# A hybrid decoder block on one core: first partial w2 sums stored from ScalarE's queue, rope tables one stretch later and wholly on VectorE, latent weights split earlier

## The chip, the cores and the metric

The kernel runs on one core of a Trainium2 chip. TensorE (PE) multiplies, VectorE (DVE) and ScalarE (ACT) prepare its operands and read its sums, GpSimd (POOL) and SyncE (SP) mostly issue transfers. The metric is the device time of one execution in microseconds; the reported time is the median of several executions.

## The reference, cut to what matters

One layer: a gated FFN, a mixer (latent attention beside a short convolution), and a second gated FFN, each behind an RMS norm modulated by an adaLN vector and each added to the residual. x is 512 x 1024 in f32; the FFN's inner width is 2816 (22 tiles of 128).

```python
h = modulate(x, norm_w[l, 0], mod[:, 0, 0], mod[:, 0, 1])
x = x + 0.5 * mod[:, 0, 2][:, None, :] * swiglu(h, ffn_w13[l, 0], ffn_w2[l, 0])
h = modulate(x, norm_w[l, 1], mod[:, 1, 0], mod[:, 1, 1])
y = hybrid_mixer(h, cos, sin, w_in[l], ...)        # starts with h @ w_in; its first columns are the latents
x = x + mod[:, 1, 2][:, None, :] * y
...
cos, sin = rope_tables(positions)                  # used in the mixer alone
```

## The kernel before, in words

All products run in f32 precision as three matmuls of split operands: `split_to` makes a rounded high part on ACT (L112) and the rest on DVE (L113). Every weight that PE multiplies by has first been loaded by SP into a raw tile and then split by these two lines.

An FFN (`ffn`) is a list of jobs that `run` goes through: while the body of job i issues PE's work, the splits of job i+1 (`prep`) are woven in at its yields, and the loads of job i+2 (`load`) are issued at its start. The first three of the 22 inner tiles are done ahead of the list; a `pair_job` does one of the others from the two w13 tiles with seven products; it needs sums of weight parts, and it gets two of these by accumulating loads on POOL's queue (L537, L538) on top of parts that SP loaded (L536). A `down_job` multiplies by w2. The inner tiles come in three phases; in the first FFN they are 0 to 5, 6 to 13 and 14 to 21, and after each phase comes a w2 stretch of eight output tiles. The first stretch stores its partial sums to a scratch array `yd` (L676 copy on ACT, L680 store), the second adds to them by an accumulating store (L678), the last fetches them back and puts the sum into the residual (`Residual.put`, L368). In the last stretch of the first FFN the output tiles 4 to 7 are done for the first half of the rows and then for the second half, with their split weights kept, so that the norm of the next part (`Norm.add`, `rstd`, `spread`, `chunk`) can start on the first half while PE is at the second.

Beside this run the adaLN products on DVE (L199), whose weights come in 1 MB blocks (L227). `rope_tables` (L740 to L779) is called in the first w2 stretch after tile 0: a scaling of one column, 20 small DVE instructions, two sines on ACT, and eight multiplications on POOL (L777). The weights of the mixer's first product (the latents, `w_c`) are loaded and split after the whole FFN in the program text (L809 to L815). Then the mixer starts with `latent_products(0)` (L840) and the norm's second half.

SBUF is cut into 17 blocks of 8 KB per partition (tag `block`), five slots of 2 KB (`slot`), ten tiles of 4 KB (`wide`) and others. Tiles of one tag take turns: a load waits until the one that it replaces was last read. A `block` holds, among others, a weight load of a job, 1 MB of adaLN weights, two activations, a split latent weight, and `rope_tmp`. The order of each engine's instructions is set ahead of time by the framework's planner, from the program's order, the data that they need and the tiles that are free; on the chip every engine then goes through its list in that order.

Of the kernel before, what the change touches and what calls it, by code (L numbers as in the profile page):

```python
# [9 lines left out]
F32R = mybir.dt.float32r  # L10
# [3 lines left out]
ALU = mybir.AluOpType  # L14
# [44 lines left out]
def tile_hybrid_block(ctx, tc, xT, pack0, pack1, pos, ada01, ada, w13f0, w13f1, w13a, w13b, w2, w_c, w_cg, w_uq, w_ukv,  # L59
# [17 lines left out]
    def block(name, dt=F32):  # L77
        return act.tile([P, 4 * T], dt, tag="block", name=name, bufs=NBLOCK)
# [28 lines left out]
    def cols(pair, c0, n):  # L107
        return tuple(t[:, c0 : c0 + n] for t in pair)
# [6 lines left out]
    def raw_load(src, n, name):  # L115
        raw = wide(f"wr_{name}") if section["kind"] == "ffn" else short("wr", WMAX, f"wr_{name}")
        nc.sync.dma_start(out=raw[:, :n], in_=src)
        return raw
# [367 lines left out]
    def first_raw(i, early):  # L486

        n = FIRST[i] * 2 * P
        per = (4 * T if early else WMAX) // n
        for k in range(KD):  # L490
            if k % per == 0:
                t = block(f"wfr{i}_{k}") if early else wide(f"wfr{i}_{k}")
            raw = t[:, k % per * n : (k % per + 1) * n]
            nc.sync.dma_start(out=raw, in_=(w13f0, w13f1)[i][k])
            yield raw

    def ffn(i, norm, spans, chunk, res, next_norm, pace, raws):
        a_pieces = {}
        ab = []
        yd = dram.tile([KD, P, T], F32, name=f"yd{i}")  # L500
# [118 lines left out]
        def down_job(phase, ms, halves, keep=False):  # L619


            f0, f1 = PHASES[i][phase]
            n = f1 - f0
            final = phase == len(PHASES[i]) - 1
            name = f"d{i}_{phase}_{ms[0]}_{halves[0]}"
            first_half = halves[0] == 0

            def load(w):
                if not first_half:
                    return  # L630
                w["raw"] = block(f"wd{name}")
                for z, m in enumerate(ms):
                    nc.sync.dma_start(out=w["raw"][:, z * WMAX : z * WMAX + n * P], in_=w2[i, m][:, f0 * P : f1 * P])
                if final:
                    for m in ms:
                        res.fetch(m)
                        nc.sync.dma_start(out=res.part[m], in_=yd[m])

            def prep(w):
                if not first_half:  # L640
                    return
                if not final:
                    ada_load(ADA[i][phase])
                elif ms[0] == 0:
                    res.room()
                for z, m in enumerate(ms):
                    raw = w["raw"][:, z * WMAX : z * WMAX + n * P]
                    if keep:
                        b = block(f"{name}_{m}", F32R)
                        kept[m] = b[:, : n * P], b[:, WMAX : WMAX + n * P]  # L650
                        split_to(*kept[m], raw)
                    else:
                        split_wide(w, raw, (m,), f"{name}_{m}", False)
                    yield
                if final:
                    for m in ms:
                        nc.vector.scalar_tensor_tensor(out=res.xin[m], in0=res.part[m], scalar=mod_col(res.v, m),
                                                       in1=res.xin[m], op0=ALU.mult, op1=ALU.add)

            def body(w):  # L660
                for m in ms:
                    ps = mm(f"{name}_{m}")
                    wt = w.get(m) or kept[m]
                    if not first_half and next_norm is not None:
                        for _ in range(next(pace_of)):
                            next(next_norm.steps, None)
                    for k in range(n):
                        for h in halves:
                            c = h * HALF
                            mm3(ps[:, c : c + HALF], cols(wt, k * P, P), cols(a_pieces[f0 + k], c, HALF),  # L670
                                k == 0 and h == halves[0], k == n - 1 and h == halves[-1])
                        if k == n // 2:
                            yield
                    if not final:
                        y = slot(f"y{name}_{m}")
                        nc.scalar.copy(out=y, in_=ps)  # L676
                        if phase:
                            nc.gpsimd.dma_start(out=yd[m], in_=y, accum_op=ALU.add)  # L678
                        else:
                            nc.gpsimd.dma_start(out=yd[m], in_=y)  # L680
                        ada_step(ADA[i][phase] // len(ms))
                        if i == phase == m == 0:
                            rope_tables()
                    else:
                        c, k = halves[0] * HALF, len(halves) * HALF
                        res.put(m, ps[:, c : c + k], c, k)
                        if next_norm is not None:
                            next_norm.add(m, c, k)
                            if m == KD - 1:
                                drain(next_norm.steps)  # L690
                                next_norm.steps = next_norm.prepare(c // P, k // P)
                    yield

            return load, prep, body
# [44 lines left out]

    def rope_tables():  # L740
        nc.vector.tensor_scalar(out=wq96, in0=wq96, scalar1=SCALE, scalar2=None, op0=ALU.mult)
        rope_tmp = block("rope_tmp")

        def rope_tile(i):
            return rope_tmp[:, 64 * i : 64 * i + 64].rearrange("p (b f) -> p b f", f=16)

        posf = rope_tmp[:, 448 : 448 + NB]
        nc.vector.tensor_copy(out=posf, in_=pos_i)
        ang = rope_tile(0)
        for b in range(NB):  # L750
            nc.vector.tensor_scalar(out=ang[:, b, :], in0=invf, scalar1=posf[:, b : b + 1], scalar2=None, op0=ALU.mult)
        TWO_PI = 6.283185307179586
        C1, C2 = 6.28125, 0.0019340515136718750
        C3 = TWO_PI - C1 - C2
        MAGIC = 12582912.0
        trig = {}
        for name, quarter in (("sin", 0.0), ("cos", 0.25)):
            kk = rope_tile(1 + 3 * len(trig))
            nc.vector.tensor_scalar(out=kk, in0=ang, scalar1=1.0 / TWO_PI, scalar2=quarter, op0=ALU.mult, op1=ALU.add)
            nc.vector.tensor_scalar(out=kk, in0=kk, scalar1=MAGIC, scalar2=None, op0=ALU.add)  # L760
            nc.vector.tensor_scalar(out=kk, in0=kk, scalar1=MAGIC, scalar2=None, op0=ALU.subtract)
            r = rope_tile(2 + 3 * len(trig))
            nc.vector.scalar_tensor_tensor(out=r, in0=kk, scalar=-C1, in1=ang, op0=ALU.mult, op1=ALU.add)
            nc.vector.scalar_tensor_tensor(out=r, in0=kk, scalar=-C2, in1=r, op0=ALU.mult, op1=ALU.add)
            nc.vector.scalar_tensor_tensor(out=r, in0=kk, scalar=-C3, in1=r, op0=ALU.mult, op1=ALU.add)
            if quarter:
                nc.vector.tensor_scalar(out=r, in0=r, scalar1=TWO_PI / 4, scalar2=None, op0=ALU.add)
            nc.vector.tensor_scalar(out=r, in0=r, scalar1=3.1415925, scalar2=-3.1415925, op0=ALU.min, op1=ALU.max)
            tb = rope_tile(3 + 3 * len(trig))
            nc.scalar.activation(out=tb, in_=r, func=AF.Sin)  # L770
            trig[name] = tb

        for nm, w in (("q", wqr_sb), ("k", wkr_sb)):
            for fn in ("cos", "sin"):
                tb = const.tile([P, NB, DR], F32, name=f"rt_{nm}{fn}")
                for j in range(2):
                    nc.gpsimd.tensor_tensor(out=tb[:, :, 16 * j : 16 * j + 16], in1=trig[fn], op=ALU.mult,  # L777
                                            in0=w[:, 16 * j : 16 * j + 16].unsqueeze(1).to_broadcast([P, NB, 16]))
                rope_tab[nm, fn] = tb  # L779

# [21 lines left out]
    x2d = dram.tile([KD, P, T], F32, name="x2d")  # L802
    r1 = Residual(1, xT, 2, x1d)
    n1 = Norm(1, r1.tiles)
    ffn(0, n0, ((0, T),), first_chunk, r1, n1, (0, 2, 3, 3), first_raw(0, False))

    wc = []  # L809
    for u in range(4):  # L810
        raw = raw_load(w_c[u], 2 * CPROJ, f"wc{u}")
        hl = block(f"wc{u}", F32R)
        hl = hl[:, : 2 * CPROJ], hl[:, 2 * CPROJ : 4 * CPROJ]
        split_to(*hl, raw[:, : 2 * CPROJ])
        wc += [cols(hl, i * CPROJ, CPROJ) for i in range(2)]  # L815
    enter("mixer")
    kr_raw = act.tile([P, NB, DR], F32, name="kr_raw")
    cst = act.tile([P, NB, 4], F32, name="cst")
# [426 lines left out]
```

## Time and profile before

| | us |
|---|---|
| median of 3 runs | 1089.38 (1087.56 to 1100.96) |
| the profiled execution | 1097.2 |
| its span, first to last instruction | 1095.4 |
| PE busy in it | 1046.0 |
| mean granted clock of PE | 0.991 |

Of the profiled execution 1.8 us lie outside its span. The profiled execution is 7.8 us longer than the median of the runs. The rows below are from that one execution; their times are in microseconds from the span's start. In its order of work the first FFN's first w2 stretch lies at about 99 to 132 us, its second at 220 to 264, its third at 345 to 389, and the mixer starts at 389.5.

### The profile page before, as it was taken

What the parts mean: (1) busy time and instruction counts of PE and PEld (TensorE: products, weight loads), DVE (VectorE), ACT (ScalarE), POOL (GpSimd) and SP (SyncE); (2) the same over time, 40 slices, a digit from 0 to 9 for tenths busy, and PEclk for the clock granted to TensorE, in tenths of its full rate; (3) what the DMA queues carried; (4) which work ended last, traced back from release to release, by engine and by line L of the source; (5) the groups of instructions that cost most, each with busy time, mean ns of one, the idle gap of its engine ahead of it and who ended that gap; (6) DMA issues with size and microseconds to landing.
All of it is one profiled execution on the core that took longest, in us unless ns stands there. A gap on an engine that the chain in (4) does not pass through costs nothing.

```text
span 1095.4 us, 19960 instructions
## 1 busy us (share of the span) xinstructions
PE 1046.0 (95%) x7870; PEld 982.7 (90%) x7870; DVE 782.3 (71%) x1326; ACT 513.9 (47%) x877; POOL 135.7 (12%) x169
## 2 busy tenths in 40 slices
PE   2999989999999989999999989899999999999997
PEld 1999989999999988888887868688999999999997
DVE  6899389855987577767468677648997488834863
ACT  7964345423554154554334433327764255524530
POOL 0001311013100112110000000001101220022001
PEclk9999999999999989999999999899999999999999
DMA  9766987579945423212245486725866894778352
GB/s 367 249 191 197 267 246 206 193 178 272 238 122 205 152 101 97 83 54 68 78 151 187 131 297 235 242 95 155 211 196 223 231 248 128 210 138 216 99 195 85
DMA packets 82254, 198.08 MB, mean 181 GB/s; under 512 B 9584, under 2 KB 12528, under 8 KB 79088
## 3 DMA queue, kind: packets, MB, share of 16 engines
q1 hardware_dynamic: 66256, 164.30, 44.8%
q0 software_dynamic: 15904, 32.51, 15.3%
q8 instruction: 61, 1.00, 0.4%
q14 instruction: 33, 0.27, 0.1%
HBM read 178.95 MB, written 17.83 MB: 180 GB/s over the span
## 4 chain that ended last, share of the span: by engine, by line
PE 76%; DVE 10%; DMA 7%; issue 3%; ACT 1%; SPq 1%; POOL 1%; POOLq 0%; DVEq 0%; ACTq 0%
PE g L134 6%; PE g L135 6%; PE g L136 6%; PE d L135 6%; PE d L136 6%; PE d L134 6%; PE u L134 5%; PE u L135 5%; PE u L136 5%; DMA sa<-in_w13a_dram 2%; DMA wr_ada<-in_ada_dram 2%; DVE ada_acc L199 2%; PE pf L135 1%; PE pf L136 1%; PE pf L134 1%
## 5 line engine op out<-in xcount | busy, mean ns | idle before, releaser
L135 PE MATMUL d<-a,d_h 128*128 128x256 f32 x616 | 171.4, 278 | 1.6 <-DVE a L113 1.6
L136 PE MATMUL d<-a,d_l 128*128 128x256 f32 x616 | 170.9, 278 | 0.0
L134 PE MATMUL d<-a,d_h 128*128 128x256 f32 x616 | 170.9, 278 | 0.0
L134 PE MATMUL u<-T,w_h 128*128 128x256 f32 x456 | 127.8, 280 | 4.0 <-ACT s L567 4.0
L135 PE MATMUL u<-T,w_h 128*128 128x256 f32 x456 | 127.3, 279 | 0.0
L136 PE MATMUL u<-T,w_l 128*128 128x256 f32 x456 | 127.2, 279 | 0.0
L112 ACT CAST w_h<-sa 128x1024 fp32r<-128x1024 f32 x76 | 79.8, 1050 | 81.7 <-issue 48.5
L135 PEld LDWEIGHTS d<-a,d_h 128*128 128x128 f32 x616 | 115.7, 188 | 2.1 <-DVE a L113 2.1
L136 PEld LDWEIGHTS d<-a,d_l 128*128 128x128 f32 x616 | 116.0, 188 | 0.0
L134 PEld LDWEIGHTS d<-a,d_h 128*128 128x128 f32 x616 | 115.9, 188 | 0.0
L113 DVE TENSOR_TENSOR w_l<-sa,w_h 128x1024 fp32r<-128x1024 f32 x76 | 92.5, 1220 | 20.5 <-ACT w_h L112 10.8
L134 PEld LDWEIGHTS u<-T,w_h 128*128 128x128 f32 x456 | 86.2, 189 | 4.9 <-ACT s L567 4.8
L136 PEld LDWEIGHTS u<-T,w_l 128*128 128x128 f32 x456 | 86.7, 190 | 0.0
L135 PEld LDWEIGHTS u<-T,w_h 128*128 128x128 f32 x456 | 86.1, 189 | 0.0
L134 PE MATMUL g<-h,w_h 128*128 128x256 f32 x304 | 84.6, 278 | 0.0
L135 PE MATMUL g<-h,w_h 128*128 128x256 f32 x304 | 84.4, 278 | 0.0
L136 PE MATMUL g<-h,w_l 128*128 128x256 f32 x304 | 84.4, 278 | 0.0
L112 ACT CAST d_h<-wdd 128x1024 fp32r<-128x1024 f32 (+1 forms) x42 | 41.0, 978 | 57.6 <-issue 31.3
L547 DVE TENSOR_TENSOR sb<-sa 128x512 f32<-128x512 f32 x38 | 26.0, 684 | 53.7 <-DMA sa<-in_w13a_dram 32.6
L113 DVE TENSOR_TENSOR d_l<-wdd,d_h 128x1024 fp32r<-128x1024 f32 (+1 forms) x42 | 47.7, 1135 | 16.8 <-ACT d_h L112 11.2
L113 DVE TENSOR_TENSOR w_l<-sb,w_h 128x1024 fp32r<-128x1024 f32 x38 | 46.4, 1220 | 17.5 <-PE g L136 13.5
L136 PEld LDWEIGHTS g<-h,w_l 128*128 128x128 f32 x304 | 57.4, 189 | 0.0
(362 smaller groups left out, 3131.6 us busy)
## 6 DMA issues: line engine op xcount, KB each, us to landing
ada<-in_ada_dram SPq DMA_DIRECT2D x24, 1024.0 KB, 6.7
sa<-in_w13b_dram SPq DMA_DIRECT2D x80, 256.0 KB, 5.0
sa<-in_w13a_dram SPq DMA_DIRECT2D x72, 256.0 KB, 5.3
wdd<-in_w_dram SPq DMA_DIRECT2D x32, 512.0 KB, 4.7
wr_ada<-in_ada_dram SPq DMA_DIRECT2D x24, 512.0 KB, 5.1
sa<-in_w13b_dram POOLq DMA_DIRECT2D x40, 256.0 KB, 6.1
sa<-in_w13a_dram POOLq DMA_DIRECT2D x36, 256.0 KB, 6.3
yd<-yd POOLq DMA_DIRECT2D x32, 256.0 KB, 6.1
```

Of the source, the lines that this page charges most:

```text
L112: nc.scalar.copy(out=hi, in_=src)
L113: nc.vector.tensor_tensor(out=lo, in0=src, in1=hi.bitcast(F32), op=ALU.subtract)
L134: nc.tensor.matmul(ps, a[0], b[0], start=first, stop=False, skip_group_check=parts)
L135: nc.tensor.matmul(ps, a[0], b[1], start=False, stop=False, skip_group_check=parts)
L136: nc.tensor.matmul(ps, a[1], b[0], start=False, stop=last, skip_group_check=parts)
L199: nc.vector.scalar_tensor_tensor(out=acc, in0=src, scalar=c, in1=acc, op0=ALU.mult, op1=ALU.add)
L547: nc.vector.tensor_tensor(out=b[:, 0], in0=a[:, 3], in1=a[:, 1], op=ALU.add)
```

## The change

Three edits, all of them in the first FFN or in `ffn`, which the second FFN uses too.

- The stores of the first w2 stretch (both FFNs, eight each) are issued by ACT instead of POOL.
- `rope_tables` is called one w2 stretch later (the first FFN's second, after tile 0); its scratch is a `slot` instead of a `block`; its eight last multiplications go from POOL to DVE.
- The latent weights' loads and splits become a generator that the FFN steps: after each of the four first-half `put`s of the last stretch one weight tile is split; the four loads come at the first step.

```diff
-    def ffn(i, norm, spans, chunk, res, next_norm, pace, raws):
+    def ffn(i, norm, spans, chunk, res, next_norm, pace, raws, tail=iter(())):
...
                         if phase:
                             nc.gpsimd.dma_start(out=yd[m], in_=y, accum_op=ALU.add)
                         else:
-                            nc.gpsimd.dma_start(out=yd[m], in_=y)
+                            nc.scalar.dma_start(out=yd[m], in_=y)
                         ada_step(ADA[i][phase] // len(ms))
-                        if i == phase == m == 0:
+                        if i == 0 and phase == 1 and m == 0:
                             rope_tables()
                     else:
                         c, k = halves[0] * HALF, len(halves) * HALF
                         res.put(m, ps[:, c : c + k], c, k)
+                        if len(halves) == 1 and first_half:
+                            next(tail, None)
...
-        rope_tmp = block("rope_tmp")
+        rope_tmp = slot("rope_tmp")
...
-                    nc.gpsimd.tensor_tensor(out=tb[:, :, 16 * j : 16 * j + 16], in1=trig[fn], op=ALU.mult,
+                    nc.vector.tensor_tensor(out=tb[:, :, 16 * j : 16 * j + 16], in1=trig[fn], op=ALU.mult,
...
-    ffn(0, n0, ((0, T),), first_chunk, r1, n1, (0, 2, 3, 3), first_raw(0, False))
     wc = []
-    for u in range(4):
-        raw = raw_load(w_c[u], 2 * CPROJ, f"wc{u}")
-        hl = block(f"wc{u}", F32R)
-        hl = hl[:, : 2 * CPROJ], hl[:, 2 * CPROJ : 4 * CPROJ]
-        split_to(*hl, raw[:, : 2 * CPROJ])
-        wc += [cols(hl, i * CPROJ, CPROJ) for i in range(2)]
+    def latent_weights():
+        raws = [raw_load(w_c[u], 2 * CPROJ, f"wc{u}") for u in range(4)]
+        for u, raw in enumerate(raws):
+            hl = block(f"wc{u}", F32R)
+            hl = hl[:, : 2 * CPROJ], hl[:, 2 * CPROJ : 4 * CPROJ]
+            split_to(*hl, raw[:, : 2 * CPROJ])
+            wc.extend(cols(hl, i * CPROJ, CPROJ) for i in range(2))
+            yield
+
+    ffn(0, n0, ((0, T),), first_chunk, r1, n1, (0, 2, 3, 3), first_raw(0, False), latent_weights())
```

## Rows read from the trace of the kernel before

**Rows 1.** The page, part 1: PE's busy time, share of the span, instructions.

```profile
PE 1046.0 (95%) x7870; PEld 982.7 (90%) x7870; DVE 782.3 (71%) x1326; ACT 513.9 (47%) x877; POOL 135.7 (12%) x169
```

**Rows 2.** Windows: stretch, length, busy us by engine, PE's clock, DMA share, GB/s.

```profile
85.00:103.00 18.00, 17.68 (x156) 17.48 (x155) 16.64 (x36) 7.80 (x12) 0.00 (x0) 1.00 0.56 191
122.00:135.00 13.00, 13.00 (x113) 13.00 (x113) 5.04 (x6) 6.27 (x10) 5.04 (x8) 1.00 1.02 288
146.00:149.60 3.60, 0.00 (x0) 0.00 (x0) 2.85 (x6) 0.86 (x2) 0.00 (x0) 1.00 1.02 315
149.60:153.40 3.80, 3.79 (x19) 3.79 (x20) 2.15 (x3) 1.57 (x2) 0.79 (x1) 0.55 1.08 309
...
103.00:135.00 32.00, 32.00 (x275) 32.00 (x274) 15.35 (x29) 11.55 (x19) 14.26 (x22) 1.00 0.90 262
```

**Rows 3.** Chain that ended last, 90 to 160: start, us, what.

```profile
114.28 12.51 DMA sa<-in_w13a_dram
...
148.27 0.35 DVE g L585
...
149.29 0.27 ACT s L567
149.61 0.47 PE u L134
```

**Rows 4.** Timeline of DVE: start, length, instruction, [idle before, what ended it].

```profile
122.49 0.69 DVE L547 TENSOR_TENSOR sb<-sa 128x512 f32<-128x512 f32 x1 [9.18 <-DMA sa<-in_w13a_dram]
...
135.08 0.69 DVE L547 TENSOR_TENSOR sb<-sa 128x512 f32<-128x512 f32 x1 [3.00 <-DMA sa<-in_w13a_dram]
```

**Rows 5.** Timeline of POOL.

```profile
111.11 0.94 POOL L537 DMA_DIRECT2D sa<-in_w13a_dram  x1
```

**Rows 6.** Timeline of SP's queue.

```profile
97.16 0.33 SPq L227 DMA_DIRECT2D ada<-in_ada_dram  x1
103.28 1.75 SPq L536 DMA_DIRECT2D sa<-in_w13a_dram  x4
...
110.59 0.33 SPq L227 DMA_DIRECT2D ada<-in_ada_dram  x1
```

**Rows 7.** Waits of SP's queue: us in total, times, longest.

```profile
SPq L227 <- POOL rt_kcos L777: 3.1, 1, 3.1
```

**Rows 8.** Tile rope_tmp: ns min/median/max, first to last start.

```profile
L763 DVE SCALAR_TENSOR_TENSOR rope_tmp<-rope_tmp x2: 210/210/211, 104.2 to 104.4; 128x64 f32<-128x64 f32 x2
...
L777 POOL TENSOR_TENSOR rt_kcos<-pk,rope_tmp x2: 768/769/770, 109.1 to 109.8; 128x64 f32<-128x64 f32 x2
```

**Rows 9.** Line L536: SP's issues, ns min/median/max.

```profile
L536 SPq DMA_DIRECT2D sa<-in_w13a_dram x72: 327/430/1812, 40.6 to 300.0; - x72
```

**Rows 10.** Windows of the second w2 stretch and of the second FFN's first.

```profile
225.00:240.00 15.00, 15.00 (x130) 15.00 (x129) 3.94 (x5) 3.45 (x5) 4.42 (x5) 1.00 0.92 173
...
845.00:885.00 40.00, 40.00 (x356) 40.00 (x355) 21.37 (x28) 13.23 (x19) 12.71 (x17) 1.00 0.91 261
```

**Rows 11.** Windows at the end of the first FFN and the mixer's start.

```profile
368.00:380.00 12.00, 12.00 (x102) 12.00 (x102) 5.01 (x10) 1.67 (x4) 2.16 (x4) 1.00 0.24 88
...
389.80:392.20 2.40, 0.06 (x1) 0.00 (x0) 2.40 (x6) 2.40 (x5) 0.54 (x1) 0.98 0.00 0
392.20:399.40 7.20, 7.14 (x23) 6.88 (x24) 4.00 (x7) 0.55 (x2) 0.71 (x1) 0.53 0.64 239
```

**Rows 12.** Tile wc: the splits' ns min/median/max, first to last start.

```profile
L112 ACT CAST wc<-wr_wc x4: 870/872/882, 387.2 to 391.0; 128x832 fp32r<-128x832 f32 x4
L113 DVE TENSOR_TENSOR wc<-wr_wc,wc x4: 1011/1015/1015, 391.2 to 395.1; 128x832 fp32r<-128x832 f32 x4
```

**Rows 13.** Timeline of PE at the mixer's start.

```profile
389.51 0.35 PE L134 MATMUL pc<-wc,h 128*128 128x416 f32 x1
392.25 0.71 PE L135 MATMUL pc<-wc,h 128*128 128x416 f32 x1 [2.40 <-DVE wc L113]
...
394.50 0.85 PE L282 MATMUL ps_ss<-ones_c,nacc 128*128 128x1 f32 x4
```

**Rows 14.** Timeline of DVE at the mixer's start.

```profile
392.51 0.41 DVE L275 TENSOR_TENSOR nacc<-nacc,sq 128x256 f32<-128x256 f32 x1
```

## What the change should do to the time

> **What bounds the kernel now.** I read the busy times first: PE is busy 1046.0 of 1095.4 us [rows 1]. So only PE's gaps, and its time at the lower clock, can be won; everything else is work that PE has to do. I then cut the span into windows and looked only for those in which PE's busy time is below the window's length or its clock below 1. Leaving aside the opening, which the change does not touch, two of them lie where the diff works.
>
> The first is in the first FFN, behind its first w2 stretch. From 146.0 to 149.6 PE does nothing, and then it runs 3.8 us at a granted clock of 0.55, that is at 1.2 instead of 2.4 GHz for most of it [rows 2]. The loss is 3.6 + 3.8 x 0.45 = 3.6 + 1.7 = 5.3 us. The chain of waits says why: PE waited for ACT's copy `s`, ACT had been held by DVE's `g`, and DVE reached `g` only at 148.27 because it was working off a backlog [rows 3]. The backlog came from waiting: DVE stood several times in front of L547 for w13 parts, 9.2 us the first time and 3.0 the last, and from 135 on it had all the postponed splits to do at once [rows 4]. The parts were late at their source. SP could issue the first pair's parts at 103.28 only, the next adaLN block at 110.59, and the load that is on the chain left at 114.28 and took 12.5 us [rows 3, 6]. Here two things of the rope tables show. The adaLN load at 110.59 was released by POOL's last rope multiplication [rows 7]: `rope_tmp` held one of the 17 blocks. And POOL, whose multiplications went on to 110.5 [rows 8], issued the first accumulating load at 111.11, when the parts that it adds to had been there for some microseconds [rows 5].
>
> A control stands in the same trace: the second FFN goes through the same lines, with the same stores on POOL and no rope tables, and PE is busy 40.0 of 40 us there [rows 10]. So I put this gap down to the block and to POOL's time, more than to the stores themselves.
>
> The second place is the mixer's start. PE's first latent matmul is at 389.51; the next one waits 2.40 us for the low part of the first latent weight [rows 13], and then 7.2 us run at a clock of 0.53 [rows 11]. The loss is 2.3 + 7.2 x 0.47 = 2.3 + 3.4 = 5.7 us. The four splits are in the text behind the FFN, and they run at 387.2 to 396.1, in the middle of the norm's work [rows 12].
>
> **The change part by part.**
>
> *Rope tables out of the first stretch.* Gone from there: eight POOL multiplications, of which the last took 0.77 us each, and some 20 small DVE instructions of about 0.21 us, 20 x 0.21 = 4.2 us in all [rows 8]. The block comes free for the loads that follow it. If every load moves up by one turn, the first pair's parts take the place of the adaLN load at 97.16 instead of 103.28, 6.1 us earlier, and the adaLN load that waited for rope is free of that wait [rows 6, 7]. The DMA engines were at a share of 0.56 in 85 to 103 and of 1.02 in 122 to 135 [rows 2], so what moves up goes into emptier time. The stall that has to be made up is 3.6 us; the source moves by 3 to 6. I take it as gone, 3.6 us, and with it the low clock, 1.7. Bounds: nothing (if the planner's new order puts another wait in front of the splits), and 5.3.
>
> *Rope tables in the second stretch.* The same 4.2 us on DVE plus eight multiplications. No row shows these on DVE; the nearest is the scratch's own two-operand instruction of the same size, 0.21 us, and on POOL they took 0.77 [rows 8]. So 1.7 us, at most 6.2. Together 5.9 us; DVE is idle 11 of 15 us there (225 to 240) and PE has no gap [rows 10]. I cost it at nothing. If they come just behind, they push work into the next wait for w13 parts. The scratch takes one of five slots for about 10 us, of which two hold adaLN sums; two are left for the partial sums, which come one in 5 us. Behind a sum's copy that found no slot, ACT's next cast would wait.
>
> *Stores on ACT.* Eight issues in each FFN leave POOL and go into ACT's list, each behind the copy that it stores, so it waits for nothing else. No row shows an issue on ACT. SP's issues took 0.33 to 1.81 us, median 0.43 [rows 9]; I take the median, 3.4 us for eight, bounds 2.6 and 14.5. What is queued behind it is ACT's next cast for a pair. ACT is busy 11.6 of 32 us in the first stretch [rows 2] and 13.2 of 40 in the second FFN [rows 10], so I cost them at nothing up to the point that is worked out below. What is won: POOL's accumulating loads no longer stand in line with stores. It is part of the 5.3 us and not added to it.
>
> The Trainium skill, page "DMA: Bandwidth & Descriptors", section "Issuing engines are not separate DMA queues", speaks against this edit: transfers from all issuing engines run on the same 16 DMA engines and interleave, and issuing from more engines saves only the time of the issue. By that rule alone the stores give nothing beyond POOL's issue time, and the first gap stays unless the loads themselves move. The share of 1.02 agrees with it [rows 2].
>
> *Latent splits earlier.* Four casts of 0.87 us and four subtractions of 1.01 us [rows 12] go from the mixer's start into 368 to 380, where DVE is busy 5.0 of 12 us and ACT 1.7 [rows 11]. They fit (4.1 more on DVE, 3.5 on ACT), and PE has no gap there: nothing. If that room were gone, they would cost what they cost now. At the mixer's start PE then goes on without the 2.4 us and without the low clock. What is late next is the second half's norm: PE's sum `ps_ss` comes after seven latent matmuls. The six behind the gap took 2.25 us at half clock [rows 13], so at full clock PE is there at 389.86 + 1.13 = 391.0. It needs DVE's last `nacc`, which ended at 392.92 with two of the four subtractions in front of it [rows 12, 14]. So a new wait of 0 to 1.9 us; I take 1.0, since the 2.0 us of subtractions are gone and ACT's square still has to come first. Gain 5.7 - 1.0 = 4.7, between 3.8 and 5.7. It may be a bit more: everything in the mixer's start hangs on the end of the first latent product.
>
> **Sum.** 5.3 + 4.7 = 10.0 us. The profiled execution would go from 1097.2 (1.8 of it outside the span) to 1087.2. It is 7.8 us above the median of the runs; I carry the difference over to the median: 1089.4 - 10.0 = 1079.4.
>
> **Rivals.**
>
> *The engines are full anyway.* In 122 to 135 the transfers take turns at a share of 1.02 [rows 2]. If the loads, moved up, only queue in the DMA engines, or if the planner's new order sets another wait ahead of the splits, the first gap stays or moves (the second stretch now has POOL's accumulating stores and the rope tables together). Then only the mixer's start is won: 1089.4 - 4.7 = 1084.7. This is also what the page's rule gives. Against it stand the emptier time before 103 and the gapless second FFN.
>
> *The issues hold ACT.* If an issue on ACT waits for room in a full transfer queue, ACT's casts wait too. It has 32 - 11.6 = 20.4 us to spare in the first stretch [rows 2], so it decides from 20.4 / 8 = 2.6 us an issue on. At 3.5 us each, eight make 28, 7.6 us too much; PE would wait as long, and by the ratio of the first gap (5.3 lost for 3.6 waited) lose 11 us, which replaces nothing of the mixer's gain: 1089.4 + 11 - 4.7 = 1095.7, slower. For it: SP's longest issue, 1.81 us [rows 9], is not far below the point. Against it: the median is 0.43, and the eight come one in 4 us.
>
> *Only the first gap closes.* The splits move but the norm's chain holds PE as long as before, low clock included: 1089.4 - 5.3 = 1084.1. Against it: PE's wait names the split [rows 13].
>
> *More than that.* The mixer's first loads wait for the last reads of the FFN's tiles; if they come earlier too, another 3 to 5 us go, some 1075.
>
> **How the numbers follow.** Forecast, both gaps closed: 0.57. Full engines or a moved gap: 0.2. Only the first gap: 0.07. ACT held: 0.06. More: 0.1. The range takes in the forecast with its bounds, the two half gains and the larger one with some 1.5 us for the scatter of a median (the three runs differ by 1.8 without the highest): 1073 to 1088; the case of ACT held is left out. A measurement of this kernel can tell about 2%, 21.8 us, from no change. All of PE's idle time in the span is 49.4 us [rows 1], much of it in the opening, so faster by over 2% has 0.01; slower by over 2% lies beyond the worst case worked out, 0.02; within 2%: 0.97.
>
> **What would show it.** In the changed profile: SP's loads of the first pair at about 97 instead of 103; POOL's first accumulating load soon behind; no wait of DVE near 9 us at L547; PE without a gap from 140 to 155 and the clock at 1. Rope on DVE between 225 and 250 with PE gapless. Latent splits between 366 and 380; PE with less than 2 us of gaps from 389 to 396 at clock 1. The prediction is wrong if a gap of PE over 3 us stands anywhere from 100 to 300, or if the clock falls behind 389.

## The result, and the profile after

| | us |
|---|---|
| before, median of 20 runs | 1093.12 (1086.19 to 1105.61) |
| changed, median of 20 runs | 1086.09 (1080.77 to 1095.84) |
| ratio | 0.9934, 95% interval 0.9914 to 0.9953 |
| the profiled execution of the changed kernel | 1089.12, span 1087.4 |

The change makes the kernel faster by 0.66%, 0.0066 x 1093 = 7.2 us, between 5.1 and 9.4. Forecast were 10.0 us, a ratio of 0.9908. The median lies in the range and the sign is right, but one of the two gaps is still there. (The forecast's 1079.4 started from 1089.4 for the kernel before; in the runs beside the changed kernel that one measured 1093.1.) The page of the changed kernel, busy times and the queue that the change adds (packets, MB, share of 16 engines):

```profile
PE 1039.0 (96%) x7870; PEld 976.2 (90%) x7870; DVE 783.1 (72%) x1334; ACT 514.4 (47%) x877; POOL 122.4 (11%) x145
...
q10 hardware_dynamic: 2304, 4.20, 1.0%
```

POOL has lost 24 instructions, 8 multiplications and 16 stores, and 13 us [rows 1]; the 16 stores are on the new queue, which is ACT's. Windows of the changed kernel, with the columns of rows 2:

```profile
122.00:135.00 13.00, 13.00 (x117) 13.00 (x116) 2.88 (x4) 5.84 (x9) 1.75 (x2) 1.00 0.86 242
140.00:145.00 5.00, 4.04 (x36) 3.84 (x34) 5.00 (x8) 1.98 (x2) 1.22 (x2) 1.00 0.83 247
145.00:150.00 5.00, 0.84 (x4) 0.84 (x5) 4.30 (x8) 1.26 (x3) 0.51 (x1) 0.67 1.03 317
150.00:155.00 5.00, 5.00 (x31) 5.00 (x31) 2.11 (x3) 1.93 (x4) 1.70 (x2) 0.65 1.07 349
225.00:240.00 15.00, 15.00 (x135) 15.00 (x134) 7.65 (x31) 4.35 (x7) 3.77 (x5) 1.00 0.78 148
270.00:275.00 5.00, 3.90 (x35) 3.71 (x34) 4.25 (x8) 2.27 (x5) 0.00 (x0) 1.00 1.06 307
368.00:380.00 12.00, 11.86 (x100) 11.65 (x98) 7.54 (x14) 3.89 (x7) 3.13 (x5) 1.00 0.43 141
...
385.00:390.00 5.00, 5.00 (x37) 4.97 (x36) 4.84 (x13) 3.27 (x7) 1.08 (x2) 1.00 0.57 184
390.00:395.00 5.00, 5.00 (x30) 4.96 (x29) 1.22 (x5) 2.51 (x10) 1.54 (x2) 1.00 0.08 29
```

**The mixer's start is repaired.** PE is busy 10.0 of 10 us from 385 to 395, at clock 1, where before it stood for 2.3 us and then ran 7.2 us at 0.53 [rows 11]. The first latent weight's tile shows it in one line for each kernel: the first and the last of these 32 matmuls (times behind the durations). The kernel before:

```profile
L134 PE MATMUL pc<-wc,h x32: 348/352/694, 389.5 to 425.1; 128*128 128x416 f32 x32
```

The changed kernel, with the casts and subtractions of the four weights:

```profile
L134 PE MATMUL pc<-wc,h x32: 348/352/537, 387.6 to 416.2; 128*128 128x416 f32 x32
...
L112 ACT CAST wc<-wr_wc x4: 871/880/882, 364.9 to 369.4; 128x832 fp32r<-128x832 f32 x4
L113 DVE TENSOR_TENSOR wc<-wr_wc,wc x4: 1011/1015/1016, 366.4 to 372.2; 128x832 fp32r<-128x832 f32 x4
```

From the first to the last of them it is 28.6 us instead of 35.6. The eight instructions cost what they cost before [rows 12], 22 to 25 us earlier, where PE runs on.

**The first gap is not repaired.** PE stands 0.96 + 4.16 = 5.1 us between 140 and 150 (3.6 before) and then runs some 5 us at a clock near 0.65, mostly at 1.2 instead of 2.4 GHz. The timeline of PE at its end names the same releaser as before:

```profile
149.16 0.58 PE L134 MATMUL u<-T,w_h 128*128 128x256 f32 x1 [5.12 <-ACT s L567]
```

The timeline of DVE in the changed kernel says what did move and what did not:

```profile
114.69 0.69 DVE L547 TENSOR_TENSOR sb<-sa 128x512 f32<-128x512 f32 x1 [2.44 <-DMA sa<-in_w13a_dram]
...
125.52 0.69 DVE L547 TENSOR_TENSOR sb<-sa 128x512 f32<-128x512 f32 x1 [8.27 <-DMA yd<-yd]
...
126.13 1.22 DVE L113 TENSOR_TENSOR w_l<-sa,w_h 128x1024 fp32r<-128x1024 f32 x1
...
134.55 0.69 DVE L547 TENSOR_TENSOR sb<-sa 128x512 f32<-128x512 f32 x1 [6.60 <-issue]
...
135.89 1.22 DVE L113 TENSOR_TENSOR w_l<-sb,w_h 128x1024 fp32r<-128x1024 f32 x1
...
147.79 0.42 DVE L585 TENSOR_TENSOR g<-g,u 128x256 f32<-128x256 f32 x1
```

The first pair's sum runs at 114.7 instead of 122.5 [rows 4]. The third runs at 134.6 instead of 135.1 [rows 4]: next to nothing won. From there the backlog is the same, and `g` comes at 147.8 instead of 148.3 [rows 3]. DVE now waits 8.3 and 6.6 us in front of the second and the third sum. The name `yd<-yd` at the first of these waits is a coincidence of times: in the kept trace (the records behind the page, with their semaphores) each of the two sums waits for the semaphore of POOL's second accumulating load (L538) of its pair. The second pair's landed at 125.50, and a store began to land at 125.52; the third pair's was issued at 126.83, when the load that it adds to had landed (126.54), and landed itself at 134.47. So the third sum hangs on when the third pair's loads leave SP:

```profile
97.53 2.03 SPq L536 DMA_DIRECT2D sa<-in_w13a_dram  x4
...
104.62 0.33 SPq L227 DMA_DIRECT2D ada<-in_ada_dram  x1
106.60 9.42 SPq L536 DMA_DIRECT2D sa<-in_w13a_dram  x4
...
116.59 3.20 SPq L536 DMA_DIRECT2D sa<-in_w13a_dram  x4
```

The first pair's loads leave from 97.5 on (103.28 before, [rows 6]), POOL's first accumulating load follows at 103.34 (111.11 before, [rows 5]). But the issue of the second pair's four loads, 2.63 us in the kernel before, takes 9.42, and the third pair's leave from 116.59 on (114.28 before, [rows 3]). SP's waits between 95 and 135 (us in total, times, longest):

```profile
SPq L536 <- DMA yd<-yd: 6.9, 1, 6.9
```

SP waits 6.9 us for one of ACT's stores to land. No such wait is in the kernel before. The kept trace says where it comes from. It has for every transfer the semaphore that its landing raises, its completion counter: SP's and ACT's transfers share eight of them, POOL's use eight others, and nowhere in the span is a transfer issued before the one that last had its counter has landed. The store that ACT issued at 107.70 and the third load of the second pair have the same counter. The store landed at 115.20; the load, for which SP was free from 108.33 on, left at 115.22.

### The profile page after: what moved, and what is told of

Its sections match the earlier page's. It is cut to its first block, busy times and chain, and to the rows that moved or that the text cites. A ratio compares the mean times of both kernels' runs of the same rounds, so it can differ in the third digit from the quotient of the medians.

```text
span 1087.4 us, 19957 instructions
## 1 busy us (share of the span) xinstructions
PE 1039.0 (96%) x7870; PEld 976.2 (90%) x7870; DVE 783.1 (72%) x1334; ACT 514.4 (47%) x877; POOL 122.4 (11%) x145
## 4 chain that ended last, share of the span: by engine, by line
PE 54%; issue 9%; DMA 7%; DVE 7%; POOL 2%; ACT 1%; SPq 0%; POOLq 0%; DVEq 0%; ACTq 0%
PE d L135 4%; PE d L136 4%; PE d L134 4%; PE g L134 4%; PE g L136 4%; PE g L135 4%; PE u L134 3%; PE u L135 3%; PE u L136 3%; DMA wr_ada<-in_ada_dram 3%; DMA sa<-in_w13a_dram 2%; DVE ada_acc L199 1%; PE p_gate L136 1%; PE p_gate L134 1%; PE p_gate L135 1%
## 5 line engine op out<-in xcount | busy, mean ns | idle before, releaser
L547 DVE TENSOR_TENSOR sb<-sa 128x512 f32<-128x512 f32 x38 | 26.1, 686 | 59.2 <-DMA sa<-in_w13b_dram 25.8
L134 PEld LDWEIGHTS g<-h,w_h 128*128 128x128 f32 x304 | 57.2, 188 | 0.2 <-ACT s L572 0.2
```

Source lines behind the costliest of these rows:

```text
L134: nc.tensor.matmul(ps, a[0], b[0], start=first, stop=False, skip_group_check=parts)
L547: nc.vector.tensor_tensor(out=b[:, 0], in0=a[:, 3], in1=a[:, 1], op=ALU.add)
```

## The experiments

Theory A is the prediction's account, theory B that the first gap is set by the third pair's parts and the order of DVE's list, which no edit touches, theory C that ACT's stores hold SP's loads. All the ratios are to the kernel before in runs beside it; 0.001 is 1.1 us.

**Each edit by itself.** Three kernels have one edit each on top of the kernel before, a fourth has the latent and rope edits together, that is the changed kernel with

```diff
-                            nc.scalar.dma_start(out=yd[m], in_=y)
+                            nc.gpsimd.dma_start(out=yd[m], in_=y)
```

*The latent edit alone* (the diff's `tail` and `latent_weights`).

> The kernel before with the latent splits alone moved. If the mixer's start is all that the change won (theory B: the first gap is set by the third pair's w13 parts and by the order of DVE's list, which none of the edits touches), this kernel gains what the whole change gained, 5 to 8 us, and its trace has PE's gap of 3.6 us at 146 us as before, none from 389 to 396 us and the clock at 1 there. If the recorded account holds (theory A: rope's block and POOL's time make the first gap), it gains the forecast 3.8 to 5.7 us for the mixer's start, and the rest of the change's gain comes from the other edits.

Measured: 0.9953 (0.9927 to 0.9978), 5.1 us. The same line of the latent tile:

```profile
L134 PE MATMUL pc<-wc,h x32: 348/352/539, 388.6 to 417.1; 128*128 128x416 f32 x32
```

28.5 us again; the first gap stays (PE busy 1.14 of 5 us from 145 on). The changed kernel's 0.9934 can't be told from this: the intervals overlap, and what the other two edits add together is not settled by the times.

*The rope edit alone* (call, slot and VectorE).

> The kernel before with the rope tables alone moved (second w2 stretch, a slot for the scratch, multiplications on DVE); stores stay on POOL. Theory A: the first gap closes, 5.3 us faster, 0.5%. Theory B: the first pair's loads leave about 6 us earlier, yet the third pair's parts arrive at about 134 to 135 us as before, PE's gap at 146 us stays between 3 and 5 us, and the time is within 0.2% of before. Theory C (the stores on ACT's queue hold SP's loads, so the rope edit alone is good): as A.

Measured: 0.9964 (0.9931 to 0.9997), 3.9 us. The window and DVE's third sum:

```profile
145.00:150.00 5.00, 5.00 (x47) 5.00 (x46) 3.30 (x6) 3.04 (x6) 0.27 (x1) 1.00 1.08 299
```

```profile
131.29 0.69 DVE L547 TENSOR_TENSOR sb<-sa 128x512 f32<-128x512 f32 x1 [2.47 <-DMA sa<-in_w13a_dram]
```

With the third sum at 131.3 instead of 135.1, PE has no gap, against theory B. So the prediction's reason for this gap was sound, as long as the stores stay on POOL.

*The store edit alone* (`nc.scalar` for `nc.gpsimd` at L680).

> The kernel before with the eight stores of each first w2 stretch alone issued by ACT. Theory A: a small part of 5.3 us, since POOL no longer has stores between the accumulating loads. Theory B: nothing, within 0.2%. Theory C: SP's loads wait for stores of ACT's queue to land (6 to 7 us in the changed kernel), so the third pair's parts come later than 135 us and the gap at 146 us grows by 1 to 4 us: 0.1 to 0.5% slower.

Measured: 1.0069 (1.0039 to 1.0099), 7.6 us slower (4.3 to 10.8). Theory C alone has the sign; its 0.1 to 0.5% is at the interval's lower end. The windows of the first gap, and SP's waits over the whole span:

```profile
145.00:150.00 5.00, 0.26 (x3) 0.06 (x1) 4.40 (x7) 0.54 (x2) 0.86 (x1) 1.00 1.00 326
150.00:155.00 5.00, 4.62 (x26) 4.62 (x27) 2.44 (x4) 1.89 (x4) 1.15 (x2) 0.66 1.08 323
```

```profile
SPq L536 <- DMA yd<-yd: 13.7, 4, 7.3
```

PE stands 5.1 us here, 1.5 more than before, and SP waits 13.7 us for stores. But only 2.5 us of these are in the first FFN; the rest is in the second FFN's first w2 stretch, where PE is busy 60.0 of 60 us (825 to 885). The third sum runs at 134.3, not later than 135 as theory C has it. Behind its own stores ACT waits once, 3.4 us. The profiled execution was the fastest of the twelve (1093.75, their median 1100.36), so where most of the 7.6 us goes no trace here shows.

*Latent and rope, stores on POOL.*

> The changed kernel with the stores back on POOL. Theory C: no load of SP waits for a store, the third pair's parts arrive some 4 to 7 us earlier, and the first gap closes: 5 to 7 us faster than the changed kernel, about 1.2% faster than before. Theory B: DVE's list still has the second and third pairs' sums ahead of the first pair's splits, the gap at 143 to 150 us stays above 3 us, and the time is within 2 us of the changed kernel's. Theory A: the first gap closes without the stores' edit too, about 10 us faster than before.

Measured: 0.9908 (0.9874 to 0.9943), 10.1 us, the size of the forecast. Windows, and DVE's third sum:

```profile
140.00:145.00 5.00, 4.38 (x39) 4.18 (x37) 4.97 (x8) 2.11 (x2) 0.88 (x1) 1.00 1.02 329
145.00:150.00 5.00, 3.87 (x34) 3.87 (x35) 3.43 (x5) 3.26 (x6) 0.00 (x0) 1.00 1.07 300
```

```profile
131.61 0.69 DVE L547 TENSOR_TENSOR sb<-sa 128x512 f32<-128x512 f32 x1 [3.57 <-DMA sa<-in_w13a_dram]
```

SP's loads of the third pair, and POOL's first accumulating load:

```profile
112.67 1.88 SPq L536 DMA_DIRECT2D sa<-in_w13a_dram  x4
```

```profile
109.02 0.90 POOL L537 DMA_DIRECT2D sa<-in_w13a_dram  x1 [0.16 <-issue]
```

PE stands 0.6 + 1.1 = 1.7 us there, and the clock stays at 1.00. The intervals of this kernel and of the changed one overlap, so the 2.9 us between the two gains (theory C said 5 to 7) are not settled by the times alone, and theory A's 10 us fit as well. The traces differ plainly: no load of SP waits for a store, the third pair's loads leave at 112.67 instead of 116.59, and its sum runs at 131.6 instead of 134.6. Theory C holds for what the stores do to SP. The other side of the store edit shows too: with the stores in line before it, POOL's first accumulating load goes out at 109.0 instead of 103.3, and the first sum runs at 120.7 instead of 114.7. What the edit wins for the first pair it loses for the third.

**The order of VectorE's list.** In the changed kernel DVE stands idle for 8.3 and 6.6 us while splits of the pair before are ready. ACT's casts for two of them, which end at 119.6 and 123.7:

```profile
118.59 1.05 ACT L112 CAST w_h<-sa 128x1024 fp32r<-128x1024 f32 x1 [2.54 <-PE d L135]
...
122.67 1.05 ACT L112 CAST w_h<-sb 128x1024 fp32r<-128x1024 f32 x1 [2.54 <-DMA sb<-in_w13a_dram]
```

DVE's halves of these splits run at 126.13 and 135.89, right behind the sums at 125.52 and 134.55: they lie behind the sum in its list. One more edge for the planner puts a pair's first sum behind the last split of the pair before it (`last_split` is set in `split_to`, `last_pair` behind a pair's last split):

```diff
+    def behind():
+        return tc.issue_after(last_pair[0].ins) if last_pair[0] is not None else nullcontext()
...
-                nc.vector.tensor_tensor(out=b[:, 0], in0=a[:, 3], in1=a[:, 1], op=ALU.add)
+                with behind():
+                    nc.vector.tensor_tensor(out=b[:, 0], in0=a[:, 3], in1=a[:, 1], op=ALU.add)
...
                 split_wide(w, sb[:, 3 * T :], ("Z4",), f"w3_{name}")
+                last_pair[0] = last_split[0]
```

It went onto four kernels. *The changed kernel:*

> The changed kernel with one more edge for the planner: the first sum of a w13 pair (the addition at L547) is put behind the last split of the pair before it on VectorE. Theory O (the order of VectorE's list makes the gap: it stands idle in front of the additions for late parts while splits that are ready lie behind them): the idle 8.3 and 6.6 us at 125.5 and 134.6 are filled with splits, PE's gap of 5.1 us near 149 and its low clock go, 5 to 7 us less than the changed kernel, ratio to before 0.987 to 0.989. Theory S (the stores hold the loads; the parts come too late in any order): the additions are as late as now, the splits before them are earlier but those of the last pair are not, gap of 3 us or more left, ratio 0.991 to 0.994, as the changed kernel.

Measured: 0.9888 (0.9831 to 0.9945), 12.2 us. DVE's sums of the second and third pair (the addition is at L553 here), and the window:

```profile
131.37 0.69 DVE L553 TENSOR_TENSOR sb<-sa 128x512 f32<-128x512 f32 x1
...
141.54 0.69 DVE L553 TENSOR_TENSOR sb<-sa 128x512 f32<-128x512 f32 x1
```

```profile
145.00:150.00 5.00, 5.00 (x46) 5.00 (x46) 3.89 (x5) 3.46 (x6) 1.73 (x2) 1.00 0.95 259
```

The sums come later than in the changed kernel, the third by 7 us, and wait for nothing; PE has no gap from 100 to 160. SP still waits for stores, up to 6.3 us here. The forecast of both theories that the sums would stay where they were was wrong, that of theory O for the gap and the time right.

*Latent, rope and the edge:*

> The changed kernel with the stores back on POOL's queue, and the same edge for VectorE's order. Theory O: the 1.8 us gap that the latent and rope edits together leave goes, ratio to before 0.988 to 0.990. Theory S: the gap is already small without the stores, and the order adds nothing, ratio 0.991 as without it. If the edge sets VectorE back elsewhere, a new gap of PE stands behind the second w2 stretch (265 to 280) and the ratio is above 0.993.

Measured: 0.9875 (0.9824 to 0.9927), 13.7 us, and no gap there. It has the lowest median of all (1081.12 beside 1093.62); that it beats the changed kernel with the edge, or the kernel without it, is inside the intervals.

*The kernel before with the edge alone:*

> The kernel before with the edge for VectorE's order alone. Theory O: the first gap (3.6 us and 3.8 us at half clock) closes without any of the three edits, 4 to 5 us, ratio 0.995 to 0.996. Theory S, and with it that the late parts make the gap (the last pair's arrive at 135 in either order): the gap stays within 1 us of 3.6, ratio 0.999 to 1.001.

Measured: 0.9957 (0.9919 to 0.9995), 4.7 us. Window and DVE's second and third sum:

```profile
145.00:150.00 5.00, 5.00 (x45) 5.00 (x44) 4.29 (x7) 3.16 (x5) 1.72 (x2) 1.00 0.89 214
```

```profile
129.77 0.69 DVE L553 TENSOR_TENSOR sb<-sa 128x512 f32<-128x512 f32 x1 [0.26 <-DMA sa<-in_w13a_dram]
...
141.74 0.68 DVE L553 TENSOR_TENSOR sb<-sa 128x512 f32<-128x512 f32 x1
```

The first gap closes with none of the three edits: the rope tables still hold their block, POOL still multiplies, the loads are as late as before (the first pair's leave from 103.79 on).

*The store edit with the edge:*

> The kernel before with the stores on ScalarE's queue and the edge for VectorE's order (a pair's first sum behind the last split of the pair before it), without the rope and latent edits. The store edit alone gave 1.0069, the edge alone 0.9957. Theory O (the held loads cost time only because VectorE stands idle at the sums with ready splits behind them): with the edge the stores cost nothing, ratio 0.994 to 0.998, PE without a gap from 140 to 155. Theory S (the held loads cost by themselves): the two effects add up, ratio 1.001 to 1.005, a gap of 3 us or more between 130 and 155.

Measured: 0.9953 (0.9914 to 0.9993). The store edit alone cost 7.6 us; with the edge no cost is left to see (0.9957 without the stores). Window, and SP's waits over the span:

```profile
145.00:150.00 5.00, 5.00 (x47) 5.00 (x46) 4.33 (x6) 3.16 (x5) 1.72 (x2) 1.00 0.96 244
```

```profile
SPq L541 <- DMA yd<-yd: 17.0, 6, 8.7
```

SP waits for stores even longer than without the edge, 17.0 instead of 13.7 us (4.8 instead of 2.5 in the first FFN), and PE has no gap from 135 to 160. So what the store edit costs hangs on DVE's order: ready work lies in its list behind a sum that waits. That it is the held loads which make the sum wait is shown for the changed kernel (the store, the third pair's loads, its sum), not for the store edit alone.

**What of a store holds the loads.** The stores stay on POOL's queue, and beside each goes one more store of a small part of the same tile on ACT's queue, with the counters that the stores of the edit alone have. First one column:

```diff
                             nc.gpsimd.dma_start(out=yd[m], in_=y)
+                            nc.scalar.dma_start(out=yt[m], in_=y[:, :1])
```

> The kernel before with its stores on POOL's queue as they were, and beside each of the sixteen one more store on ScalarE's queue, of one column of the same tile (128 elements of 4 bytes, to a scratch array that nobody reads). In the compiled program these small stores take the same turns among the eight completion counters as the stores of the edit alone. Theory S, by counters: SyncE's loads wait for the small stores as they waited for the large ones, SP's first pair is out later and the third load of the next pair waits; the gap grows, ratio 1.004 to 1.010 as with the store edit alone. Rival B (the bytes of the stores, or their way over the 16 DMA engines beside the loads, cost the time): 0.5 KB cost nothing, ratio 0.998 to 1.002 and no wait of SP for a store.

Measured: 1.0457 (1.0391 to 1.0523), 50 us slower, far off both. The column's issues and landings (min, median, max; first line: issue durations in ns):

```profile
L682 ACTq DMA_DIRECT2D yt<-yd x16: 326/326/347, 105.5 to 924.0; - x16
...
DMA to landing us min/median/max: 7.8/12.9/16.8
```

128 pieces of 4 bytes need 12.9 us to land, the whole tile of 256 KB from the same queue 5.1 (2.7 to 10.2, in the changed kernel). The transfers beside them are slower too. Those issued between 100 and 150 (KB each, median us to landing; in the kernel before 9.7 and 6.0):

```profile
sa<-in_w13a_dram SPq DMA_DIRECT2D x12, 256.0 KB, 15.3
yd<-yd POOLq DMA_DIRECT2D x5, 256.0 KB, 15.4
```

So this run doesn't separate the counters from the transfers: loads and stores beside the small pieces slow down with them. It does show that a store of 0.5 KB can cost more than one of 256 KB. The Trainium skill, page "DMA: Bandwidth & Descriptors", section "Specifications", says that below 512 B a transfer becomes a read-modify-write; 4-byte pieces that land later than 2 KB ones agree with it, though no run here shows the mechanism.

Then one row of the tile, 2 KB in one piece (`out=yt[m], in_=y[:1]`):

> The kernel before with its stores on POOL's queue, and beside each of the sixteen one more store on ScalarE's queue, of one row of the same tile (2 KB in one piece; the column of the run before was 128 pieces of 4 bytes and took 7.8 to 16.8 us to land, longer than the 2.7 to 10.2 of the whole 256 KB). Theory S (loads wait for the store that had their completion counter): such a wait is counted from the product's copy on, so it needs neither bytes nor a slow landing; SP still waits for the row stores, for 1 to 7 us in all, and the ratio is 1.002 to 1.008. Rival P (what cost time was the landing of 4-byte pieces, and the whole store's bytes in the edit): the row lands in 2 to 4 us, SP is held under 1 us, ratio 0.998 to 1.002.

Measured: 1.0006 (0.9968 to 1.0044). The same counters, and no time lost. SP has no wait for `yt` between 90 and 140; over the whole span it has one, 4.8 us before 882, where PE is busy 15.0 of 15 us (875 to 890). So a row can hold a load by its counter too, as theory S has it, but only once: by the kept trace the rows land in 1.1 to 5.0 us, and all the other loads that share a counter with a row come for it when the row has landed. Of the 1.002 to 1.008 that theory S said for the time, the interval reaches the lower part alone. That the price of sharing counters goes with how long the store takes to land fits this; it is not shown, since no run changes the counters alone and leaves the whole stores on ACT's queue.

**Which part of the rope edit.** The scratch in a slot, all else as before:

```diff
-        rope_tmp = block("rope_tmp")
+        rope_tmp = slot("rope_tmp")
```

> The kernel before with the rope scratch in a slot instead of a block; the place in the first w2 stretch and POOL's eight multiplications stay. Theory A1 (the block is what holds the loads back): SP's first pair is out at 97 to 100, the gap near 146 shrinks to under 2 us, ratio 0.995 to 0.997, nearly all of what the rope edit alone gave (0.9964). Theory A2 (the time of POOL and VectorE in the stretch is what counts): the loads move but POOL's first accumulating load is as late as before, gap within 1 us of 3.6, ratio 0.999 to 1.001.

Measured: 0.996 (0.9928 to 0.9992), 4.4 us, as much as the whole rope edit. SP's first pair and PE's window:

```profile
97.72 2.72 SPq L536 DMA_DIRECT2D sa<-in_w13a_dram  x4
```

```profile
145.00:150.00 5.00, 5.00 (x46) 5.00 (x46) 4.12 (x6) 2.60 (x4) 1.33 (x2) 1.00 1.07 338
```

POOL's eight multiplications are still in the first stretch, and PE has no gap there. Of the rope edit's parts the block is the one that counts (A1).

The call one stretch later, block and POOL kept (`if i == 0 and phase == 1 and m == 0`):

> The kernel before with the rope tables called one w2 stretch later, the scratch still a block and the eight multiplications still on POOL. Theory A (block and engines' time are both out of the first stretch, whatever happens to them in the second): the first gap closes as with the rope edit alone, ratio 0.995 to 0.998; POOL's multiplications and the block cost nothing in the second stretch, where PE has no gap. Rival: they cost there what they cost before (POOL issues the accumulating stores and loads, a load waits for the block), a gap of 2 to 4 us opens between 225 and 280, ratio 0.999 to 1.002.

Measured: 0.9966 (0.9929 to 1.0002). The first gap closes here too, and one of the same size appears in the second stretch:

```profile
265.00:270.00 5.00, 1.77 (x16) 1.57 (x15) 4.25 (x8) 0.86 (x2) 0.03 (x1) 0.90 1.05 312
270.00:275.00 5.00, 5.00 (x24) 5.00 (x25) 1.97 (x3) 1.57 (x2) 1.70 (x2) 0.50 1.02 242
```

The profile sides with the rival (3.2 us of idle time and 5 us at half clock, about what the first gap cost), the time with theory A; the interval reaches both. What the place alone gives stays open.

## Why the prediction was right and wrong

- **What bounds the kernel:** right. Both places were there to be won: 5.1 us by the latent edit, 4.7 by the edge that closes the first gap alone.
- **The time:** that the median lies in the range is in part luck. The range, 15 us wide, also held the rival with the mixer's start alone (1084.7), and that rival is nearer to 1086.1 than the forecast of 1079.4.
- **Mixer's start:** right. Forecast 4.7 us (3.8 to 5.7), measured 5.1 (2.4 to 8.0) by the latent edit alone. The term "a new wait of 0 to 1.9 us; I take 1.0" is 0: in the changed kernel `ps_ss` comes at 392.16, after 24 latent matmuls instead of the seven that the prediction took over from the trace before, and PE doesn't wait for it.
- **Rope out of the first stretch:** right by itself, 3.9 us (0.3 to 7.6) for the 5.3 forecast, and the block was rightly named first; "POOL's time" beside it had no share that shows, by the slot run.
- **Rope in the second stretch at nothing:** right in 225 to 240, where PE is busy 15.0 of 15 us. The eight multiplications took 0.22 us each on DVE, as estimated from a scratch instruction. A gap of 1.1 us at 270 is new. The rope tables' new place is not its only cause: the slot run has them in the first stretch and a gap of 1.3 us between 265 and 270. What makes it stays open.
- **The failed step: "Stores on ACT ... I cost them at nothing".** The issue was sized rightly (0.33 us for 0.43), and the rival "the issues hold ACT" falls with it: its point was 2.6 us an issue. But the step looked only at the queue that the stores were moved to and at who waits in ACT's list. It missed that SP's loads share their completion counters with ACT's transfers: in the changed kernel one store holds SP for 6.9 us, and the third sum runs 3 us later than with the stores on POOL. Alone the edit costs 7.6 us, most of it not located. The "win" beside it, POOL's accumulating loads no longer in line with stores, is there (103.3 instead of 109.0 for the first), but it comes to the first pair, which doesn't decide.
- **The second failed step: "the source moves by 3 to 6. I take it as gone".** The first pair's loads did move by 5.8 us. I took that for the whole row of pairs; the third one decides, and with the loads before it held by a store its own left at 116.59, against 112.67 with the stores on POOL. "No wait of DVE near 9 us at L547" was the sign named for it, and 8.3 us stand there.
- **The cause one level down:** the prediction read "a backlog that came from waiting" and went for the loads. The backlog came from DVE's order too: ready splits stood behind waiting sums. The edge alone closes the gap with the loads as late as ever. The control that I drew from the second FFN (same lines, no gap) excluded neither.
- **The rival "the engines are full anyway":** its time (1084.7, a gain of 4.7 us) is nearer than the forecast, its reason is not what held the loads: while SP stood at the counter (108 to 115) the share of the transfers was about 0.95, but with the latent and rope edits and the stores on POOL it was 0.95 in the same stretch too, and there no load waited for a store and the third sum ran 3 us earlier. The rule in it, of the Trainium skill's page "DMA: Bandwidth & Descriptors", section "Issuing engines are not separate DMA queues", that issuing from another engine saves only the issue, is no full account either: alone the stores on ACT made the kernel slower.

So 10.0 us were there to be had, and the latent and rope edits had them (10.1, between 6.2 and 13.8); the store edit gave some 3 back, as far as the overlapping intervals let one say. With the order of VectorE's list mended as well, 12.2 and 13.7 us are measured, which the intervals don't tell from 10.1.

## What to carry to other kernels

When a transfer is moved to another engine's queue, ask not only what stands behind its issue, but which other queue's transfers share its completion counters: here a store that took 7.5 us to land held the loads of another engine for 6.9. When an engine's list is fixed ahead, a long wait ahead of one instruction is a question about the order first: look for what is ready behind it. And where several arrivals feed one backlog, cost the last of them, not the first.

## What the runs showed of the hardware that was not expected

- 128 pieces of 4 bytes, 0.5 KB in all, took 12.9 us to land (median), where 256 KB in one store took 5.1; the loads issued beside them between 100 and 150 took 15.3 us instead of 9.7, and sixteen such stores cost the kernel 50 us.
- An issue on ACT's queue took 0.33 us, and a store on it, through a counter that it shared with a load, let SP wait up to 8.7 us (the store edit with the edge).
- With 1.7 us of idle time between 140 and 150 in the kernel with the latent and rope edits PE's granted clock stayed at 1.00; after the 5.1 us in the changed kernel it was 0.65 over the next 5 us, that is mostly 1.2 instead of 2.4 GHz.
